# A mixture-of-experts loop with TensorE's order written out as a software pipeline

## The chip, the cores and the metric

One core of a Trainium2 chip runs a whole two-part transformer in float32. The metric is the device time of one execution in microseconds, from the core's first instruction to its last. The kernel before was run three times.

## The reference

The program is a first block (two layers with attention mixers and a dense feed-forward part) and a second block of two layers, each with a mixer and then sixteen experts. The change lies only in the experts of the second block. Sequence length there is L = 272 (256 tokens and 16 meta tokens), the width 1024, an expert's inner width 1408. Each expert takes the 34 tokens that score highest for it (expert choice), scaled by their score:

```
cap = EC_FACTOR * L // N_EXPERTS                 # 2 * 272 // 16 = 34
aff = jax.nn.softmax(jnp.einsum("bld,de->ble", u, router).astype(jnp.float32), axis=-1)
gates, idx = lax.top_k(jnp.swapaxes(aff, 1, 2), cap)
xs = jax.vmap(lambda ub, ib: ub[ib])(u, idx)
hid = jax.nn.silu(jnp.einsum("becd,edf->becf", xs, w1)) * jnp.einsum("becd,edf->becf", xs, w3)
ys = jnp.einsum("becf,efd->becd", hid, w2) * gates[..., None].astype(u.dtype)
return jax.vmap(lambda yb, ib: jnp.zeros((L, D), yb.dtype).at[ib].add(yb))(ys, idx)
```

The three weight matrices of an expert are read once from HBM; nothing is shared between experts.

## The kernel before

`second_block` keeps the residual x in SBUF, features on the partitions (8 chunks of 128 x 272). After each layer's mixer, `experts` (line 2185) computes the router, the 34 slots per expert as one-hot matrices `oh`, and the tokens with tokens on the partitions (`utok`, `utl`). Its loop (line 2364) then runs over the sixteen experts in four groups of four.

`gather` (line 2276) multiplies `utok` and `utl` with the one-hot matrices of a group and writes the group's tokens, scaled by the norm's gain, into one of two halves of `mixT` (`xs` in the code). It runs at once for a whole group before the group's first expert: 24 products in two rounds of two PSUM banks, each evicted by ScalarE or VectorE.

`one_expert` (line 2314) then does, in the order of the code:

- three parts j of the two up projections, 512, 512 and 384 columns wide. The gathered tokens (34 columns) are the stationary operand, the weight slabs the moving one; w1 goes to PSUM partitions 0 to 33, w3 to 64 to 97 of the same bank. ScalarE copies the one half to `hid` (line 2328), VectorE the other (line 2329);
- right behind each part, 3 or 4 transposes of `hid` on TensorE (`K.tr`, helper line 440), silu on ScalarE (2336) and the product on VectorE (2337) into `hT`;
- two small products that spread the slots and scores of the expert over the partitions (`sp`, `ap`), from which `pe`, the weighted one-hot matrix, is made (2343, 2345);
- the down projection: 11 row chunks, two products each, from three slabs (4, 4 and 3 chunks), evicted to `ys` (2354, 2355);
- the scatter: eight products of `ys` with `pe`, each added to a chunk of x by VectorE (2360). After the last expert each chunk of x is also squared on ScalarE (1208), and a product with ones adds the squares to `nst`, the sums that the next norm needs.

All products are issued through the helper at line 388, so the profile's lines are read by the names of their tiles: `bank<-w,mixT` is an up projection, `bank<-ca,hid` a transpose, `bank<-slT,ca` and `bank<-affT,ca` the two small products, `bank<-w,hT` the down projection, `bank<-pe,ys` the scatter, `bank<-oh,utok` and `bank<-oh,utl` the gather.

The weights come through `weights` (2303): every slab goes to the next slot of its size, seven slots of 2 MiB (`big`, lines 2390 to 2393, two of them in halves with a transfer each) and three of 1.5 MiB (`small`, line 2394). An expert uses six big and three small slabs. All are issued by SyncE from one queue (line 378), each waits until TensorE has read the slab that was in its slot, and none overtakes another. In layer 1's last expert the last slab comes in three pieces of 512 KB.

PSUM tiles come from one pool of eight banks. The order of each engine's instructions is set by the framework's scheduler; a `manual_schedule` around a piece of code keeps the named engines in the order of the code. In the mixers TensorE is held so; in the experts' loop nothing is (MS is 1, so the branch at the loop's head is not taken).

Of the kernel before, what the change touches and what calls it, by code (L numbers as in the profile page):

```python
# [2 lines left out]
L, S, D, KD = 272, 256, 1024, 8  # L3
# [24 lines left out]
# columns of the first mixer's input projection in units of 128, in the order of their use  # L28
# [3 lines left out]
# the second mixer's projections as w_in2 holds them  # L32
# [3 lines left out]
# mixer chunks in four passes of the output projection  # L36
# [104 lines left out]
def prep(I):  # L141
# [50 lines left out]
    for l in range(2):  # L192
        # two chunks of both halves to a slab
        for j in range(11):
            c = slice(256 * j, 256 * j + 256)
            fu.append(_slab(np.concatenate([up[l][:, :FF][:, c], up[l][:, FF:][:, c]], 1)).reshape(128, -1))
# [96 lines left out]
class Fill:  # L293
    """Work for the tensor engine that is handed out in small steps while another chain waits."""
# [26 lines left out]
    def piece(self):  # L321
        """one step; what it takes, or None when there is none to be had."""
# [18 lines left out]
class Kit:  # L341
# [15 lines left out]
    def widen(self, ctx, name, n, side="left", ring=None, size=4096, parts=1):  # L357
        """n more slots for the weight stream while ctx lasts, in one or more parts."""
# [23 lines left out]
    def load(self, src, n=4096):  # L382
        """a slab in the next slot."""
# [6 lines left out]
    def mm3(self, out, a, b, start=True, stop=True):  # L390
        """a^T b from exact two-part splits: high x high, high x low, low x high."""
# [4 lines left out]
    def split(self, src, a, into=None):  # L396
        """weights [128, a, b] as the exact sum of two parts of twelve significant bits."""
# [9 lines left out]
    def units(self, thunks, ahead=1):  # L407
        """split weights in turn, some units ahead of their use."""
# [7 lines left out]
    def cols(self, src, ms, nk=KD, width=512):  # L416
        """thunks for the 128-column chunks ms of a slab that is loaded at the first of them."""
# [9 lines left out]
    def rows(self, src):  # L427
        """thunks for pairs of the 128-row chunks of a slab of 512 columns."""
# [27 lines left out]
    def add_squares(self, st, k, sq):  # L456
        """adds the k-th of eight chunks of squares, over its features, to the token sums of column group k % 4."""
# [3 lines left out]
    def token_sums(self, st, tiles, g4):  # L461
        """the four groups' sums -> 32 x the sums with the tokens on the partitions, a column per tile."""
# [7 lines left out]
def first_block(K, tap):  # L470
# [5 lines left out]
    with ExitStack() as cx:  # L476
# [65 lines left out]
        def spread(r):  # L542
            """two columns of per-token values -> rows on all partitions, in PSUM [128, S]."""
# [8 lines left out]
        def pair_sums(st, p, src, dve=False):  # L552
            """adds the squares of the chunk pair p to the token sums."""
# [11 lines left out]
        def scale_of(st):  # L565
            """token sums -> 1 / rms on all partitions, in PSUM [128, S]."""
# [14 lines left out]
        def bank_out(st, z, p, bank, gp):  # L581
            """token sums of the squares of bank p, two 128-feature chunks, and the chunks times gp."""
# [6 lines left out]
        def post_norm(st, z, last=False):  # L589
            """x += z / rms(y), y of token sums st; the token sums of the new x."""  # L590
# [16 lines left out]
        def fm(us, hT, emit, n=4, nk=KD):  # L607
            """feature-major products for n units of 128 columns, two to a bank; emit(i, bank) per bank."""
# [21 lines left out]
        def tok_v(us, hT, dst):  # L630
            """token-major products [S, 512]: activations stationary, weights moving."""
# [25 lines left out]
        def scores_soft(sc_ps, G, n, biases, scale):  # L657
            """scores of G heads [128, G, n] in one PSUM bank -> normalised probabilities in SBUF."""
# [19 lines left out]
        def pv_heads(h, pr, v, heads, hh, o_ps):  # L678
            """o^T of heads 2 j + hh, j in heads (pairs of this bank), for query half h."""
# [15 lines left out]
        def o_out(oT, o_ps, m0, h):  # L695
            """the outputs of four head pairs for query half h, split."""
# [5 lines left out]
        def attend(score, bias, scale, v, base, oT, m0, waits):  # L702
            """softmax attention of four head pairs, the scores a step ahead of the rest."""
# [32 lines left out]
        def even_mixer(hT, oT, cy, bias):  # L736
# [42 lines left out]
        def odd_mixer(hT, oT, cy, c1v):  # L779
# [17 lines left out]
            def stick_a(zps, az):  # L797
                """scores and exp(-|scores|) of a step, a part per half of the heads."""
# [1631 lines left out]
```

## Time and profile before

| | us |
|---|---|
| median of 3 runs | 2753.06 |
| lowest, highest run | 2749.35, 2765.5 |
| profiled execution, span | 2750.4 |
| expert loop of layer 0, first product to last down product | 670.2 |
| expert loop of layer 1, likewise | 671.8 |
| TensorE busy, share of the span | 2482.9, 90% |
| VectorE busy, share of the span | 1084.4, 39% |
| ScalarE busy, share of the span | 755.7, 27% |

The profiled execution's own time is its span; it lies 2.7 us under the median. A busy matmul in the profile is not TensorE at its peak, since matmuls overlap and their ends are modelled; each float32 product appears as two records. PE is TensorE, PEld its weight load, DVE VectorE, ACT ScalarE, SP SyncE. "granted clock" or PEclk is the share of TensorE's full 2.4 GHz that it was given.

### The profile page before, as it was taken

To read this page: it belongs to the slowest core of one execution; us is meant where nothing else is said; L and a number is where in the kernel's file an instruction comes from. 1 tells how busy PE (TensorE), PEld (TensorE's weight loads), DVE (VectorE), ACT (ScalarE), POOL (GpSimd) and SP (SyncE) were. 2 spreads that over 40 slices of the span, in tenths; PEclk is the share of its full clock that TensorE was granted. 3 is DMA by queue.
4 is the path that set the end of the run, shared out by engine and by line. 5 is a ranking of instruction groups with operands and counts; after the bars stand their busy time and mean duration, and the time that the engine had idled before them with its cause. 6 is when DMAs were issued, how large, how long until landed. Compare 5 with 4: busy or idle time off the path is not lost. (4 is left out here: it accounts for less than half of the span.)

```text
span 2750.4 us, 43569 instructions
## 1 busy us (share of the span) xinstructions
PE 2482.9 (90%) x18599; PEld 1515.0 (55%) x18599; DVE 1084.4 (39%) x2308; ACT 755.7 (27%) x1471; POOL 206.9 (8%) x260
## 2 busy tenths in 40 slices
PE   6999998999989998898888988899988898888987
PEld 4779987689978784232232322588762232322322
DVE  3557766577675562111111111474641111111112
ACT  3445545355554341000010000342420000000001
POOL 0011011110032110000000000122100000000000
PEclk9999999999988999999999999898989999999998
DMA  9484443764132337999999998223169999999992
GB/s 360 161 370 179 171 160 118 314 268 154 45 94 63 117 135 301 425 425 380 422 381 426 414 392 353 86 69 117 71 241 397 424 388 425 386 389 423 388 425 100
DMA packets 78194, 753.43 MB, mean 274 GB/s; under 512 B 9600, under 2 KB 13584, under 8 KB 24624
## 3 DMA queue, kind: packets, MB, share of 16 engines
q1 hardware_dynamic: 75072, 748.38, 67.4%
q8 instruction: 146, 2.39, 0.3%
q10 hardware_dynamic: 2928, 2.26, 0.3%
q14 instruction: 48, 0.39, 0.0%
HBM read 749.54 MB, written 1.07 MB: 273 GB/s over the span
## 5 line engine op out<-in xcount | busy, mean ns | idle before, releaser
L388 PE MATMUL bank<-w,mixT 128*34 128x512 f32 (+1 forms) x3072 | 643.2, 573 | 0.0
L388 PEld LDWEIGHTS bank<-w,mixT 128*34 128x34 f32 x3072 | 176.7, 114 | 409.6 <-issue 393.9
L403 DVE TENSOR_TENSOR wlo<-w,whi 128x1024 fp32r<-128x1024 f32 (+1 forms) x242 | 298.9, 1237 | 168.6 <-ACT whi L401 167.3
L401 ACT ACTIVATE whi<-w 128x1024 fp32r<-128x1024 f32 x246 | 258.4, 1054 | 319.8 <-PE bank L388 125.5
L388 PE MATMUL bank<-w,hT 128*34 128x512 f32 x1408 | 330.8, 628 | 0.0
L2329 DVE COPY hid<-bank 34x512 f32<-34x512 f32 (+1 forms) x96 | 62.4, 650 | 627.7 <-ACT hid L2328 627.7
L388 PE MATMUL up<-hF,whi 128*128 128x256 f32 x1408 | 256.6, 285 | 5.2 <-ACT hF L573 5.2
L2328 ACT ACTIVATE hid<-bank 34x512 f32<-34x512 f32 (+1 forms) x96 | 53.2, 555 | 690.3 <-PE bank L388 690.3
L388 PEld LDWEIGHTS up<-hF,whi 128*128 128x128 f32 x1408 | 219.7, 192 | 6.8 <-ACT hF L573 5.9
L388 PEld LDWEIGHTS bank<-w,hT 128*34 128x34 f32 x1408 | 84.4, 117 | 229.9 <-issue 223.3
L388 PE MATMUL bank<-u,whi 128*128 128x272 f32 (+1 forms) x896 | 207.3, 324 | 2.5 <-ACT u L1293 2.3
L388 PE MATMUL up<-hF,wlo 128*128 128x256 f32 x704 | 199.4, 284 | 0.0
L440 PE MATMUL bank<-ca,hid 128*128 128x128 f32 x352 | 59.5, 288 | 131.2 <-DVE hid L2329 131.2
L388 PEld LDWEIGHTS bank<-u,whi 128*128 128x128 f32 (+1 forms) x896 | 148.1, 198 | 19.6 <-issue 6.9
L440 PEld LDWEIGHTS bank<-ca,hid 128*128 128x128 f32 x352 | 36.7, 140 | 211.3 <-DVE hid L2329 211.3
L2355 DVE COPY ys<-bank 34x512 f32<-34x512 f32 x32 | 22.2, 694 | 318.7 <-ACT ys L2354 318.7
L388 PE MATMUL bank<-u,wlo 128*128 128x272 f32 (+1 forms) x448 | 136.0, 304 | 5.5 <-DVE wlo L403 3.7
L388 PEld LDWEIGHTS up<-hF,wlo 128*128 128x128 f32 x704 | 134.4, 191 | 0.2
L388 PE MATMUL bank<-pe,ys 34*128 34x272 f32 x512 | 100.3, 433 | 22.3 <-ACT ys L2354 22.1
L452 POOL TENSOR_TENSOR rr<-rv,ca 128x3 f32<-128x3 f32 (+4 forms) x28 | 32.7, 1170 | 1027.9 <-DVE rv L450 1027.9
L2354 ACT ACTIVATE ys<-bank 34x512 f32<-34x512 f32 x32 | 18.9, 590 | 316.2 <-PE bank L388 316.2
L2360 DVE TENSOR_TENSOR x<-x,bank 128x272 f32<-128x272 f32 x256 | 95.4, 433 | 23.8 <-PE bank L388 21.0
(501 smaller groups left out, 3637.1 us busy)
## 6 DMA issues: line engine op xcount, KB each, us to landing
w<-in_ew SPq DMA_DIRECT2D x136, 2048.0 KB, 14.1
w<-in_ew SPq DMA_DIRECT2D x95, 1536.0 KB, 10.6
w<-in_ew SPq DMA_DIRECT2D x112, 1024.0 KB, 12.7
w<-in_ada SPq DMA_DIRECT2D x24, 2048.0 KB, 8.3
w<-in_ffn_up SPq DMA_DIRECT2D x22, 2048.0 KB, 8.4
w<-in_w_in SPq DMA_DIRECT2D x54, 512.0 KB, 3.6
w<-in_ffn_down SPq DMA_DIRECT2D x10, 2048.0 KB, 8.5
w<-in_ab_in SPq DMA_DIRECT2D x5, 2048.0 KB, 15.4
```

The costliest lines, as they stand in the source:

```text
L388: self.nc.tensor.matmul(out, lhsT, rhs, start=start, stop=stop, skip_group_check=True)
L401: self.nc.scalar.activation(v(hi[:, :n]), src, AF.Copy)
L403: (self.nc.gpsimd if self.splits in self.pool_share else self.nc.vector).tensor_tensor(v(lo[:, :n]), src, v(hi[:, :n].bitcast(F32)), op=OP ...
L440: self.nc.tensor.transpose(out, in_, self.ident[:k, :k] if n is None else n)
L452: nc.gpsimd.tensor_tensor(r[:, :n], v[:, :n], self.cst("half")[:, :n], op=OP.pow)
L2328: nc.scalar.activation(hb[0:CAP, :n], pu[0:CAP, :n], AF.Copy)
L2329: nc.vector.tensor_copy(hb[64:64 + CAP, :n], pu[64:64 + CAP, :n])
L2354: nc.scalar.activation(ys[0:CAP], py[0:CAP], AF.Copy)
L2355: nc.vector.tensor_copy(ys[64:64 + CAP], py[64:64 + CAP])
L2360: nc.vector.tensor_tensor(x[:, k], x[:, k], pc[:, :L], op=OP.add)
```

## The change

`one_expert` is cut into functions: `up` (one part of the up projections with its copies to `hid`), `turned` (the transposes of one part with silu and product), `places` (the two small products and `pe`), `down` (the products of one slab of w2) and `scatter`. The loop calls them in a new order and holds TensorE to it with `manual_schedule`; the other engines are still ordered by the scheduler. The transposes of part 0 come behind part 1, those of part 1 behind part 2, those of part 2 behind the first slab of the down projection. The scatter of an expert comes behind part 0 of the next. `gather` does half of its work per call; both halves for group 0 stand ahead of the loop, those for a later group inside experts 1 and 2 of the group before. `nst` takes its bank after the loop instead of before it.

```diff
-            def gather(g):
+            def gather(g, k0):
                 hot = [oh[:, t, 4 * g:4 * g + 4].rearrange("p e c -> p (e c)") for t in range(3)]
-                for k0 in (0, 2):
-                    pg = [K.bank() for _ in range(2)]
+                pg = [K.bank() for _ in range(2)]
...
-            nst = K.bank("nst")
-
-            def one_expert(e):
...
+            def up(ex, e, j, n, off):
+
+                ws = [weights(A[m][l, e, :, off:off + 8 * n], 8, n) for m in ("ew1", "ew3")]
+                pu = K.bank()
...
+                nc.scalar.activation(hb[0:CAP, :n], pu[0:CAP, :n], AF.Copy)
+                nc.vector.tensor_copy(hb[64:64 + CAP, :n], pu[64:64 + CAP, :n])
+                ex["hid", j] = hb
+
+            def turned(ex, j, n):
+
+                pt, nf, hb = K.bank(), n // 128, ex.pop(("hid", j))
+                for f in range(nf):
+                    K.tr(pt[:, 128 * f:128 * f + 128], hb[:, 128 * f:128 * f + 128])
...
+            def scatter(ex, nst=None):
+
                 for n, k in enumerate((0, 4, 1, 5, 2, 6, 3, 7)):
                     r = slice(64 * (k // 4), 64 * (k // 4) + CAP)
                     pc = K.bank()
-                    K.mm(pc[:, :L], ys[r, 128 * (k % 4):128 * (k % 4) + 128], pe[r])
+                    K.mm(pc[:, :L], ex["ys"][r, 128 * (k % 4):128 * (k % 4) + 128], ex["pe"][r])
                     nc.vector.tensor_tensor(x[:, k], x[:, k], pc[:, :L], op=OP.add)
-                    if e == NE - 1:
+                    if nst is not None:
                         square_sums(K, Y.tile([128, L], F32, name="nsq"), nst, n, k)
 
-            for e in range(NE):
-                if e % 4 == 0:
-                    gather(e // 4)
-                with ExitStack() as co:
-                    if MS > 1 and e == 0:
-                        co.enter_context(tc.manual_schedule(engines={mybir.EngineType.SP}))
-                    one_expert(e)
+            offs = [8 * sum(widths[:j]) for j in range(3)]
+            prev = None
+            with tc.manual_schedule(engines={mybir.EngineType.PE}):
+                for k0 in (0, 2):
+                    gather(0, k0)
+                for e in range(NE):
+
+                    ex = {"hT": Y.tile([128, 11, CAP], F32, name="hT")}
+                    up(ex, e, 0, widths[0], offs[0])
+                    if prev is not None:
+                        scatter(prev)
+                    up(ex, e, 1, widths[1], offs[1])
+                    turned(ex, 0, widths[0])
+                    places(ex, e)
+                    up(ex, e, 2, widths[2], offs[2])
+                    turned(ex, 1, widths[1])
+                    if e % 4 in (1, 2) and e < NE - 4:
+                        gather(e // 4 + 1, 2 * (e % 4 - 1))
+                    down(ex, e, 0, 4)
+                    turned(ex, 2, widths[2])
+                    down(ex, e, 4, 4)
+                    for f0, n in ((8, 3),) if e < NE - 1 or l == 0 else ((8, 1), (9, 1), (10, 1)):
+                        down(ex, e, f0, n)
+                    prev = ex
+                nst = K.bank("nst")
+                scatter(prev, nst)
             return nst
```

On TensorE, in the kernel before, from the down projection of expert 2 of layer 0 through expert 3 to the gather of the second group, the instructions stand so:

```order
L388 MATMUL bank<-w,hT 34x512 x22
L388 MATMUL bank<-pe,ys 128x272 x8
L388 MATMUL bank<-w,mixT 34x512 x16
L440 MATMUL bank<-ca,hid_11698 128x128 x4
L388 MATMUL bank<-w,mixT 34x512 x16
L440 MATMUL bank<-ca,hid_11699 128x128 x4
L388 MATMUL bank<-w,mixT 34x384 x16
L440 MATMUL bank<-ca,hid_11700 128x128 x3
L388 MATMUL bank<-slT,ca 128x272
L388 MATMUL bank<-affT,ca 128x272
```

Then follow the 22 products of the down projection, the 8 of the scatter and the gather's 8, 4, 8 and 4. Each group of transposes reads the `hid` that the products right ahead of it have just filled.

On TensorE, in the changed kernel, expert 1 of layer 0 from the scatter of expert 0 on (its own part 0 stands right ahead):

```order
L388 MATMUL bank<-pe,ys 128x272 x8
L388 MATMUL bank<-w,mixT 34x512 x16
L440 MATMUL bank<-ca,hid_11698 128x128 x4
L388 MATMUL bank<-slT,ca 128x272
L388 MATMUL bank<-affT,ca 128x272
L388 MATMUL bank<-w,mixT 34x384 x16
L440 MATMUL bank<-ca,hid_11699 128x128 x4
L388 MATMUL bank<-oh,utok 128x136 x8
L388 MATMUL bank<-oh,utl 128x136 x4
L388 MATMUL bank<-w,hT 34x512 x8
L440 MATMUL bank<-ca,hid_11700 128x128 x3
L388 MATMUL bank<-w,hT 34x512 x14
```

Every group of transposes now has a part or a slab's products between itself and the products that filled its `hid`, and half of the next group's gather stands in the middle of the expert.

At the end of layer 0, TensorE's scatter of the last expert with the sums of squares (`nst`), in the kernel before:

```order
L388 MATMUL bank<-pe,ys 128x272
L388 MATMUL nst<-nsq,ca 32x272
L388 MATMUL bank<-pe,ys 128x272 x4
L388 MATMUL nst<-nsq,ca 32x272
L388 MATMUL bank<-pe,ys 128x272
L388 MATMUL nst<-nsq,ca 32x272
L388 MATMUL bank<-pe,ys 128x272 x2
L388 MATMUL nst<-nsq,ca 32x272 x5
```

Four of the scatter's products go ahead together in one place, and the last five sums stand at the end.

The same place in the changed kernel, with the numbers of the buffers:

```order
L388 MATMUL bank_14519<-pe_14446,ys_14515 128x272
L388 MATMUL nst_14518<-nsq_14522,ca_65 32x272
L388 MATMUL bank_14525<-pe_14446,ys_14515 128x272
L388 MATMUL nst_14518<-nsq_14528,ca_65 32x272
L388 MATMUL bank_14531<-pe_14446,ys_14515 128x272
L388 MATMUL nst_14518<-nsq_14534,ca_65 32x272
```

Five more such pairs follow: product and sum now take strict turns, eight times. SyncE issues the experts' transfers in the same order as before.

## Rows read from the trace of the kernel before

**Rows 1.** The page's rate of the transfers, in 40 equal slices of the span.

```profile
GB/s 360 161 370 179 171 160 118 314 268 154 45 94 63 117 135 301 425 425 380 422 381 426 414 392 353 86 69 117 71 241 397 424 388 425 386 389 423 388 425 100
```

**Rows 2.** Windows (stretch, length; PE, PEld, DVE, ACT, POOL busy; PEclk; DMA share; GB/s).

```profile
1065.40:1735.60 670.20, 594.16 (x2868) 203.78 (x2864) 112.34 (x262) 60.73 (x142) 1.49 (x8) 0.96 0.93 387
2053.40:2725.20 671.80, 595.72 (x2866) 204.76 (x2864) 112.13 (x261) 60.74 (x142) 0.00 (x0) 0.96 0.92 384
1100.00:1220.00 120.00, 105.63 (x509) 34.56 (x507) 20.89 (x48) 10.42 (x24) 0.00 (x0) 0.97 1.01 425
```

**Rows 3.** DMA issues of the experts' weights: times, KB each, us to landing.

```profile
w<-in_ew SPq DMA_DIRECT2D x136, 2048.0 KB, 14.1
w<-in_ew SPq DMA_DIRECT2D x95, 1536.0 KB, 10.6
w<-in_ew SPq DMA_DIRECT2D x112, 1024.0 KB, 12.7
...
w<-in_ew SPq DMA_DIRECT2D x3, 512.0 KB, 4.7
```

**Rows 4.** Timeline of TensorE, expert 0 of layer 0 (start, length, what).

```profile
1065.45 7.06 PE L388 MATMUL bank<-w,mixT 128*34 128x512 f32 x32
...
1074.02 0.66 PE L440 MATMUL bank<-ca,hid 128*128 128x128 f32 x4 [1.51 <-DVE hid L2329]
...
1083.70 5.36 PE L388 MATMUL bank<-w,mixT 128*34 128x384 f32 x32
1090.32 0.55 PE L440 MATMUL bank<-ca,hid 128*128 128x128 f32 x3 [1.27 <-DVE hid L2329]
...
1091.90 9.64 PE L388 MATMUL bank<-w,hT 128*34 128x512 f32 x44
1102.23 2.83 PE L388 MATMUL bank<-pe,ys 34*128 34x272 f32 x16 [0.69 <-ACT ys L2354]
1104.99 1.48 PE L388 MATMUL bank<-w,mixT 128*34 128x512 f32 x6
```

**Rows 5.** SyncE's waits from 1065 to 1740 us: total, times, longest.

```profile
SPq L378 <- PE bank L388: 581.5, 88, 24.5
```

**Rows 6.** TensorE's waits from 1065.4 to 1735.6 us: total, times, longest.

```profile
PE bank L440 <- DVE hid L2329: 65.6, 48, 1.5
PE bank L388 <- ACT ys L2354: 10.4, 15, 0.7
```

**Rows 7.** Windows at a loop's start, after a gather, and at its end.

```profile
1060.00:1080.00 20.00, 18.49 (x102) 8.46 (x102) 2.25 (x6) 3.43 (x7) 0.00 (x0) 0.93 0.70 270
1080.00:1100.00 20.00, 17.29 (x89) 5.71 (x87) 2.32 (x5) 2.01 (x5) 0.00 (x0) 1.00 0.87 343
...
1240.00:1260.00 20.00, 15.90 (x85) 5.41 (x81) 2.81 (x6) 2.48 (x6) 0.00 (x0) 1.00 0.86 342
...
1700.00:1720.00 20.00, 17.13 (x84) 5.10 (x82) 1.98 (x4) 1.75 (x4) 0.86 (x7) 0.97 0.43 167
```

**Rows 8.** Timeline of TensorE, second half of the second group's gather.

```profile
1230.94 2.12 PE L388 MATMUL bank<-oh,utok 128*128 128x136 f32 x16
1232.99 0.73 PE L388 MATMUL bank<-oh,utl 32*128 32x136 f32 x8
1233.65 0.63 PE L388 MATMUL bank<-w,mixT 128*34 128x512 f32 x2
```

**Rows 9.** Timeline of TensorE at the end of the layers.

```profile
1725.99 9.64 PE L388 MATMUL bank<-w,hT 128*34 128x512 f32 x44
...
2725.86 0.72 PE L388 MATMUL bank<-pe,ys 34*128 34x272 f32 x2 [0.69 <-ACT ys L2354]
...
2731.20 1.27 PE L388 MATMUL bank<-pe,ys 34*128 34x272 f32 x2
...
2733.44 1.27 PE L388 MATMUL bank<-pe,ys 34*128 34x272 f32 x2
...
2738.52 1.44 PE L388 MATMUL nst<-nsq,ca 128*32 128x272 f32 x4 [0.51 <-ACT nsq L1208]
```

More of the change, by code (lines that the diff above doesn't have):

```diff
@@ new lines, in gather @@
+                pg = [K.bank() for _ in range(2)]
+                for i in range(2):
+                    for q in range(2):
+                        k = k0 + i + 4 * q
+                        for t in range(2):
+                            K.mm(pg[i][:, 136 * q:136 * q + 136], utok[:, t, 128 * k:128 * k + 128], hot[t],
+                                 start=t == q == 0, stop=False)
+                for q in range(2):
+                    for i in range(2):
+                        j = 32 * (k0 + i)
+                        K.mm(pg[i][:, 136 * q:136 * q + 136], utl[j:j + 32, 128 * q:128 * q + 128], hot[2][j:j + 32],
+                             start=False)
@@ L2300, in experts @@
+                for q in range(2):
+                    for i in range(2):
+                        k = k0 + i + 4 * q
+                        o, ps = xs[:, g % 2, k], pg[i][:, 136 * q:136 * q + 136]
+                        if i == 0:
+                            nc.scalar.activation(o, ps, AF.Copy, scale=n2[:, k:k + 1])
+                        else:
+                            nc.vector.tensor_scalar(o, ps, n2[:, k:k + 1], None, op0=OP.mult)
             turn = [0]
@@ new lines, in up @@
+            def up(ex, e, j, n, off):
+                ws = [weights(A[m][l, e, :, off:off + 8 * n], 8, n) for m in ("ew1", "ew3")]
+                pu = K.bank()
+                r = slice(CAP * (e % 4), CAP * (e % 4) + CAP)
+                for k in range(KD):
+                    for i, w in enumerate(ws):
+                        K.mm(pu[64 * i:64 * i + CAP, :n], xs[:, e // 4 % 2, k, r], w(k), start=k == 0, stop=k == KD - 1)
+                hb = hid[turn[0] % HID]
+                turn[0] += 1
+                nc.scalar.activation(hb[0:CAP, :n], pu[0:CAP, :n], AF.Copy)
+                nc.vector.tensor_copy(hb[64:64 + CAP, :n], pu[64:64 + CAP, :n])
+                ex["hid", j] = hb
@@ new lines, in turned @@
+            def turned(ex, j, n):
+                pt, nf, hb = K.bank(), n // 128, ex.pop(("hid", j))
+                for f in range(nf):
+                    K.tr(pt[:, 128 * f:128 * f + 128], hb[:, 128 * f:128 * f + 128])
+                pv = pt[:, :n].rearrange("p (f c) -> p f c", f=nf)
+                sl = Y.tile([128, 4, CAP], F32, name="sl")
+                nc.scalar.activation(sl[:, :nf], pv[:, :, 0:CAP], AF.Silu)
+                nc.vector.tensor_tensor(ex["hT"][:, 4 * j:4 * j + nf], sl[:, :nf], pv[:, :, 64:64 + CAP], op=OP.mult)
@@ L2338, in one_expert, with places @@
+            def places(ex, e):
                 sp = K.bank()
@@ L2343, in one_expert, with down @@
                 nc.scalar.activation(ab, ap[:, :L], AF.Copy)
-                pe = Y.tile([128, L], F32, name="pe")
-                nc.vector.scalar_tensor_tensor(pe, sp[:, :L], K.cst("iotap"), ab, op0=OP.is_equal, op1=OP.mult)
-                py = K.bank()
-                for f0, n in ((0, 4), (4, 4), (8, 3)) if e < NE - 1 or l == 0 else ((0, 4), (4, 4), (8, 1), (9, 1), (10, 1)):
-                    w = weights(A["ew2"][l, e, :, f0:f0 + n].rearrange("p f n -> p (f n)"), n, 1024)
-                    for f in range(n):
-                        for i in range(2):
-                            K.mm(py[64 * i:64 * i + CAP, :], hT[:, f0 + f], w(f)[:, 512 * i:512 * i + 512],
-                                 start=f0 + f == 0, stop=f0 + f == 10)
-                ys = Y.tile([128, 512], F32, name="ys")
-                nc.scalar.activation(ys[0:CAP], py[0:CAP], AF.Copy)
-                nc.vector.tensor_copy(ys[64:64 + CAP], py[64:64 + CAP])
+                ex["pe"] = Y.tile([128, L], F32, name="pe")
+                nc.vector.scalar_tensor_tensor(ex["pe"], sp[:, :L], K.cst("iotap"), ab, op0=OP.is_equal, op1=OP.mult)
+            def down(ex, e, f0, n):
+                if f0 == 0:
+                    ex["py"] = K.bank()
+                py = ex["py"]
+                w = weights(A["ew2"][l, e, :, f0:f0 + n].rearrange("p f n -> p (f n)"), n, 1024)
+                for f in range(n):
+                    for i in range(2):
+                        K.mm(py[64 * i:64 * i + CAP, :], ex["hT"][:, f0 + f], w(f)[:, 512 * i:512 * i + 512],
+                             start=f0 + f == 0, stop=f0 + f == 10)
+                if f0 + n == 11:
+                    ys = ex["ys"] = Y.tile([128, 512], F32, name="ys")
+                    nc.scalar.activation(ys[0:CAP], py[0:CAP], AF.Copy)
+                    nc.vector.tensor_copy(ys[64:64 + CAP], py[64:64 + CAP])
+            def scatter(ex, nst=None):
                 for n, k in enumerate((0, 4, 1, 5, 2, 6, 3, 7)):
```

41 lines of the change are left out of this document (removed).

## The prediction

> **What bounds the kernel now.** I read the page's slices first: the rate of the transfers stands near 400 to 426 GB/s in two long stretches of the span and far below that elsewhere [rows 1]. Those stretches are the expert loops of the two layers of the second block, the only part that the change touches. The table of windows then gives each loop as one row: from the first product of expert 0 to the end of expert 15's last product it is 670.2 us in layer 0 and 671.8 us in layer 1, with TensorE at a granted clock of 0.96 and a mean of 387 and 384 GB/s [rows 2]. In a stretch without a gather the rate is 425 GB/s with the DMA engines busy all the time (share 1.01) [rows 2]. So two resources are nearly level here and the question is which one ends an expert.
>
> Work it out for both. The DMA issues for `in_ew` are 136 of 2048 KB, 95 of 1536, 112 of 1024 and 3 of 512 [rows 3]: 540,672 KB, or 276.8 MB per layer and 17.3 MB per expert. At 425 GB/s an expert takes 40.7 us. The timeline of TensorE in expert 0, at full clock, shows 39.5 us from its first product to the first product of expert 1 [rows 4]. The gathers of the three later groups and the half-clock stretches come on top: 670/16 is 41.9 us per expert. So TensorE's own chain is what ends an expert, by about one microsecond over the transfers. That agrees with the wait tables: SyncE waited 581.5 us for TensorE to release a weight buffer [rows 5], while TensorE's own list of waits is led by 65.6 us in 48 waits for `hid`, 1.37 us each and three per expert, and 10.4 us in 15 waits for `ys` [rows 6]: TensorE stands still while ScalarE and VectorE copy what it is about to transpose or scatter.
>
> A second cost is less visible. The buffers hold seven slabs of 2 MiB and three of 1.5 MiB, 19.4 MB, a little more than one expert. They are full when expert 0 begins. As TensorE is the slower one, they stay as full as the releases allow, and at the end of the layer the transfers stop early: from 1700 to 1720 us the rate is already 167 GB/s while products run until 1735.6 [rows 2, 7]. That drain is time in which the layer's scarcest resource does nothing.
>
> **The change, part by part.** *The waits.* Transposes stand one part later and the scatter stands behind the next expert's first part. What is between is a part of 5.4 to 7.1 us [rows 4], against copies that TensorE awaited for 1.3 to 1.5 us, or 0.7 us for `ys` [rows 4, 6]. The cover is several times the wait, so I count all three waits and the `ys` wait as gone: 3 x 1.4 + 0.7 = 4.9 us per expert, leaving 39.5 - 4.9 = 34.6 us. If a copy were late after all, what stands behind it on TensorE is one whole part. The third transpose has the thinnest cover: it stands behind the first eight products of the down projection, 8/22 of 9.64 = 3.5 us, against 1.3 [rows 4].
>
> *The gather.* The same 24 products per group now come as two halves of 12, inside experts 1 and 2 of the group before. A half took 2.7 us at full clock (1230.94 to 1233.65) [rows 8]. TensorE's work does not shrink, but the ScalarE and VectorE evictions behind it lie beside products, and TensorE no longer arrives at a new group with all releases late: after the gather at 1227 the rate fell to 342 GB/s for 20 us [rows 7]. Three gathers of 5.4 us are 16 us per layer.
>
> *TensorE's new sum* is 16 x 34.6 + 16 = 570 us per layer at full clock, against about 606 us that the transfers need (next). The order of the two is reversed: what is late next is the weight transfer, and TensorE waits for slabs.
>
> *The transfers' sum.* 276.8 - 19.4 = 257.4 MB remain at the first product, at 425 GB/s 605.7 us. They cannot begin before a buffer is released: half a slab halfway through the first part, 1065.4 + 3.5 = 1069 us. Until the pipeline of releases is full there are gaps; in the kernel before, the windows from 1060 to 1100 us run at 270 and 343 GB/s [rows 7]. With the releases of parts 1 and 2 now about 2 us earlier I put the gaps at 5 us (bounds: 0, and 11 us, the whole shortfall of these two windows against 425: 3.1 + 1.6 MB). That gives the last byte at 1069 + 605.7 + 5 = 1680 us. Behind it come the landing and the products that still stand: the last slab has 3 of 11 row chunks, 2.6 us of 9.64, and about 3 us for landing and for what TensorE has left of the slabs before (bounds 2 and 8). So the last product of layer 0 ends near 1686 instead of 1735.6: **50 us less**. The same length of 620.6 us from 2053.4 in layer 1 ends at 2674 instead of 2725.2: **51 us less** [rows 9]. The three small last slabs of layer 1 wait for part 2 of the last expert as they did; eleven microseconds of products lie over their transfer, 0.5 MB each.
>
> *The tail.* After the last expert, the scatter and the sums of squares are now in strict turn: one scatter product, then the sum that needs VectorE's add and ScalarE's square of it, then the next. Before, four scatter products went ahead in one place and two in another. A single turn took 2.24 us (2731.20 to 2733.44) [rows 9]; eight turns are 18 us, where the whole took 14.1 us (2725.86 to 2739.96) [rows 9]. This wait is added; behind it on TensorE stand all later scatter products, and the next layer or the output waits for the last. I take +4 us per layer (bounds 0, and +10 if in layer 0 VectorE's weight splitting falls between the adds).
>
> *Costs put at nothing.* The transfers are issued in the same order, so the buffers' turns do not change; the first mixer's weights of layer 1 still wait for TensorE's releases. One more PSUM bank is free during the loop, since the sums' bank is taken only at its end. ScalarE and VectorE have 61 and 112 us of work in 670 [rows 2], so their new order has slack.
>
> *Sum.* 50 + 51 - 2 x 4 = 93 us. The profiled span of 2750.4 becomes 2657. The median of the runs lies 2.7 us above that span, so I predict **2660 us**.
>
> **Two rules of the Trainium skill weighed.** The rate that carries the sum is 425 GB/s over 120 us with one core at work [rows 2]. The Trainium skill's page DMA: Bandwidth & Descriptors (section Where 436 GB/s comes from) says that loads from HBM are bound near 358 GB/s per core, and sets 435 as the fabric's ceiling. By 358 the 257.4 MB would take 719 us, more than the loop takes now, and the change could win nothing; by 435 they take 592 us and each layer ends 14 us earlier than I say. The trace disagrees with the lower figure and lies just under the upper one, so the measurement decides.
>
> The granted clock was 0.96 over the loops, so of 670 us about 54 were at half clock [rows 2], and this with TensorE never short of weights. The Trainium skill's page TensorE: Matmul & The Clock Gate (section Loop structure matters more than you think) speaks against this change: a loop that waits for a transfer before its products lets the engine fall to the lower clock. That is rival B, whose price follows from rows.
>
> **Rivals.** *A, the forecast:* the transfers end the layer. Its own range comes from 420 to 430 GB/s (about 7 us per layer either way), the gaps and the tail: 2644 to 2682.
>
> *B: the clock.* Waiting for slabs, TensorE runs at 1.2 GHz more often. At half clock, work takes twice as long; TensorE's 570 us may lose 50 us per layer before it is later than the transfers, which is 100 us at half clock, twice today's 54. Today's idle time, 670 - 594 = 76 us, made those 54 us [rows 2], and the new idle time is smaller (620 - 570 = 50 us, some 3 us per expert, spread over nine slabs); when the clock falls, the waits vanish and with them the cause. If it lost 75 us instead, the layers would end 25 us later each: 2710.
>
> *C: the queue runs dry.* SyncE issues in one order, and the loads of part 2 wait for part 2 of the expert before, with others behind them. If this left gaps so that the mean was 405 GB/s, the transfers would take 30 us more per layer: 2720. Against it: 425 was held for 120 us at a time with the same order and later releases.
>
> *D, slower:* once TensorE is starved, each slab's landing and its products follow one another instead of overlapping, because the hand-made order lets nothing pass the waiting product. An expert then costs 40.7 us plus what is uncovered. It decides from 1.2 us per expert (41.9 now); three uncovered waits of 1.5 us would be 45.2 us and 53 us per layer more: about 2870. Against it: ten slots ahead keep the queue filled when TensorE is the one that waits.
>
> **How the numbers follow.** A 0.79, B 0.09, C 0.07, D 0.03, and 0.02 that the transfers were the limit already and nothing changes. What can be told from no change here is about 1%, 27 us. A and most of B and C are faster by more: 0.93 faster, 0.04 the same, 0.03 slower. The range holds A and a good part of B and C: 2643 to 2705.
>
> **What would show it.** In the profile after: waits for `hid` and `ys` nearly gone from TensorE's list and waits for `in_ew` in their place, some 40 us or more per layer; the rate at 425 GB/s without the dips after gathers and until about 6 us before the last product; loops of about 620 us; the last scatter with its sums about 18 us. I am wrong if the clock in the loops falls below 0.9, if the rate stays under 410 with SyncE waiting for releases throughout, or if `hid` still leads the waits.

## The result and the profile after

| | before | after |
|---|---|---|
| median of 4 runs, us | 2751.2 | 2675.68 |
| lowest, highest run, us | 2748.42, 2765.5 | 2670.22, 2680.31 |
| profiled execution, span, us | 2750.4 | 2668.5 |
| mean granted clock of the span | 0.942 | 0.948 |

The ratio is 0.9709, with a 95% interval of 0.9675 to 0.9743: faster by 2.9%. The forecast was 2660 us in a range of 2643 to 2705; the median lies in it, 16 us above the forecast. The rate of the transfers, in the page's 40 slices, is the first thing to look at:

```profile
GB/s 366 145 366 221 174 167 127 267 301 190 20 106 73 114 81 229 389 426 424 426 426 424 425 425 425 157 81 55 92 233 372 425 425 424 426 425 425 426 424 166
```

In [rows 1] the two loops show 380, 381, 392, 388, 386, 389 between slices of 425. Now every slice that lies wholly in a loop, behind its first, stands at 424 to 426, and the rate falls away at once behind it. The windows after give the two loops, two stretches inside the first, the tails behind the loops, the end of the second loop's transfers, and the mixer between the loops (columns as in [rows 2]):

```profile
1065.40:1686.60 621.20, 582.27 (x2868) 197.59 (x2864) 112.33 (x262) 60.26 (x142) 1.55 (x8) 0.98 1.00 418
2011.10:2632.50 621.40, 582.19 (x2867) 199.30 (x2864) 112.04 (x261) 60.25 (x142) 0.00 (x0) 0.97 0.99 415
1100.00:1220.00 120.00, 120.00 (x635) 43.60 (x632) 26.10 (x62) 13.00 (x31) 0.00 (x0) 1.00 1.01 425
1240.00:1260.00 20.00, 17.14 (x74) 5.26 (x76) 3.66 (x9) 0.59 (x1) 0.00 (x0) 0.83 1.01 427
1686.60:1712.30 25.70, 17.03 (x32) 4.99 (x32) 6.49 (x11) 5.95 (x12) 0.18 (x1) 0.58 0.29 97
2626.00:2628.00 2.00, 2.00 (x12) 0.59 (x12) 0.26 (x1) 0.26 (x1) 0.00 (x0) 1.00 0.35 143
2628.00:2630.00 2.00, 2.00 (x12) 0.59 (x10) 0.00 (x0) 0.00 (x0) 0.00 (x0) 1.00 0.00 0
2632.50:2658.20 25.70, 17.03 (x32) 4.99 (x32) 4.19 (x9) 4.09 (x10) 0.00 (x0) 0.58 0.00 0
1712.30:2011.10 298.80, 276.68 (x3634) 234.15 (x3634) 187.00 (x446) 124.51 (x283) 59.68 (x74) 0.90 0.33 120
```

The loops went from 670.2 and 671.8 us to 621.2 and 621.4. From 1100 to 1220 us TensorE did 635 records' work where it did 509 [rows 2], without an idle moment in the profile, while the transfers ran at the same 425 GB/s. Then the transfers took over: from 1240 to 1260 us, behind the first gather's old place, the rate holds 427 where it was 342 [rows 7], and TensorE is the one with gaps. At the end of layer 1, where no later layer's weights are in the queue, the transfers last into the window from 2626 to 2628 us, 5 to 6 us ahead of the end of the last product at 2632.5. Before, the rate was down to 167 GB/s from 1700 to 1720 us, with 16 us of the loop still to come [rows 7].

The waits of TensorE after, from 1065 to 1690 us (total, times, longest):

```profile
PE bank L388 <- DMA w<-in_ew: 38.9, 19, 4.6
PE nst L388 <- ACT nsq L1208: 1.0, 1, 1.0
PE bank L388 <- ACT ys L2359: 0.7, 1, 0.7
```

The 48 waits for `hid` are gone, and so are the `ys` waits of the loop; the one left belongs to the tail [rows 6]. TensorE now waits for weights instead: 582.3 us busy and 38.9 us waiting are the loop's 621.2. SyncE's waits in the same stretch:

```profile
SPq L378 <- DMA w<-in_ew: 406.0, 123, 5.0
SPq L378 <- PE bank L388: 140.7, 38, 24.5
```

SyncE waited 581.5 us for TensorE's releases [rows 5]; now it is 140.7, and it waits 406.0 us for earlier transfers: buffers come free faster than the transfers can use them. Accordingly each transfer spends longer in the queue (KB each, us from issue to landing):

```profile
w<-in_ew SPq DMA_DIRECT2D x136, 2048.0 KB, 28.3
w<-in_ew SPq DMA_DIRECT2D x95, 1536.0 KB, 27.1
w<-in_ew SPq DMA_DIRECT2D x112, 1024.0 KB, 28.5
```

Against 14.1, 10.6 and 12.7 us [rows 3] the landings take twice as long or more, at a rate that is no lower.

Inside an expert the timeline of TensorE (1447 to 1473 us: end of part 0, scatter of the expert before, part 1, transposes of part 0, part 2, transposes of part 1, start of a gather) reads:

```profile
1447.28 7.05 PE L388 MATMUL bank<-w,mixT 128*34 128x512 f32 x30 [1.75 <-DMA w<-in_ew]
1454.27 2.10 PE L388 MATMUL bank<-pe,ys 34*128 34x272 f32 x16
1456.30 7.06 PE L388 MATMUL bank<-w,mixT 128*34 128x512 f32 x32
1463.30 0.65 PE L440 MATMUL bank<-ca,hid 128*128 128x128 f32 x4
1464.99 5.36 PE L388 MATMUL bank<-w,mixT 128*34 128x384 f32 x32
1470.28 0.65 PE L440 MATMUL bank<-ca,hid 128*128 128x128 f32 x4
1470.77 2.02 PE L388 MATMUL bank<-oh,utok 128*128 128x136 f32 x16
```

Neither the scatter nor the transposes carry a wait any more; in [rows 4] the transposes waited 1.51 and 1.27 us and the scatter 0.69. The one bracket left names a slab.

Where did the 81.9 us of the span come from? The loops gave 49.1 and 50.5. The tails, from the last down product to the last sum, took 25.65 us each instead of 14.1 and 14.8: 11.5 and 10.9 us given back. The mixer of layer 1 between the loops took 298.8 instead of 303.6 us, though nothing in it was changed. 49.1 + 50.5 - 11.5 - 10.9 + 4.8 is 82.0.

What was open then: whether the transfers are what ends the loop now; which of the three moves the loop's gain needs; and why the tail cost three times the forecast.

### The profile page after: what moved, and what is told of

Read it like the earlier page. It is cut to its first block, busy times and chain, and to the rows that moved or that the text cites. A ratio compares the mean times of both kernels' runs of the same rounds, so it can differ in the third digit from the quotient of the medians.

```text
span 2668.5 us, 43625 instructions
## 1 busy us (share of the span) xinstructions
PE 2462.9 (92%) x18599; PEld 1502.2 (56%) x18599; DVE 1084.4 (41%) x2308; ACT 755.4 (28%) x1471; POOL 207.2 (8%) x260
## 5 line engine op out<-in xcount | busy, mean ns | idle before, releaser
L388 PE MATMUL bank<-w,mixT 128*34 128x512 f32 (+1 forms) x3072 | 683.2, 578 | 78.1 <-DMA w<-in_ew 78.1
L388 PEld LDWEIGHTS bank<-w,mixT 128*34 128x34 f32 x3072 | 188.3, 115 | 540.0 <-issue 402.9
L388 PE MATMUL bank<-w,hT 128*34 128x512 f32 x1408 | 314.6, 595 | 0.0
L388 PEld LDWEIGHTS bank<-w,hT 128*34 128x34 f32 x1408 | 77.8, 112 | 189.2 <-issue 187.3
L388 PE MATMUL acc<-gh,wlo 128*128 128x256 f32 x352 | 99.1, 282 | 0.0
L388 PE MATMUL acc<-gh,whi 128*128 128x256 f32 x352 | 99.0, 281 | 0.0
L388 PE MATMUL acc<-gl,whi 128*128 128x256 f32 x352 | 99.0, 281 | 0.0
L388 PE MATMUL bank<-hT,whi 128*128 128x256 f32 (+1 forms) x464 | 88.9, 294 | 7.7 <-ACT hT L573 3.1
```

The source lines that it names most:

```text
L388: self.nc.tensor.matmul(out, lhsT, rhs, start=start, stop=stop, skip_group_check=True)
```

## The experiments

Each takes the changed kernel and edits one thing. Where single executions are compared, the loops are compared and not the totals, since the changed kernel's own runs differ by 10 us. "Loop" is the stretch from the first up product to the last down product.

**no_scatter.** If TensorE no longer ends an expert, work taken from it must gain nothing.

```diff
                     up(ex, e, 0, widths[0], offs[0])
-                    if prev is not None:
-                        scatter(prev)
                     up(ex, e, 1, widths[1], offs[1])
```

> Leaves out the scatter of experts 0 to 14 with its adds to x; only expert 15 is scattered. TensorE has 15 x 2.8 = 41 us less to do per layer. Theory (the transfers end the loop): the loops stay at 621 us within 3, the waits for weights grow by about 40 us per layer. Rival (TensorE's work still ends the loop): the loops fall to 580 to 590 us, the span by 60 to 80.

Measured: 2673.17 us, loops of 623.3 and 623.7. Window and wait of layer 0's loop:

```profile
1064.60:1687.90 623.30, 560.59 (x2626) 176.96 (x2624) 67.99 (x142) 60.56 (x142) 1.55 (x8) 0.95 0.99 416
```

```profile
PE bank L388 <- DMA w<-in_ew: 62.0, 28, 5.3
```

240 records of TensorE's work are gone and the loop is no shorter. TensorE's busy time fell by 21.7 us, and its waits for weights rose by 23.1 us, from 38.9 to 62.0. That is little more than half of the 40 us expected: a scatter in the changed kernel's loop is 2.10 us long (1454.27 above) and not the 2.8 of the kernel before, 15 of them 31.5 us, and the granted clock fell too, 0.98 to 0.95, so that the work left took longer. The loop is not TensorE's to shorten.

**fewer_bytes.** The other side of the same question: take bytes from the transfers and leave TensorE all its products.

```diff
-                w = weights(A["ew2"][l, e, :, f0:f0 + n].rearrange("p f n -> p (f n)"), n, 1024)
+                if f0 < 8:
+                    w = ex["w2"] = weights(A["ew2"][l, e, :, f0:f0 + n].rearrange("p f n -> p (f n)"), n, 1024)
+                else:
+                    w = lambda f, b=f0 - 8: ex["w2"](b + f)
```

> Leaves out the transfer of the third slab of w2 of every expert (its products read the second slab again): 25.2 MB or 59 us of transfers less per layer, TensorE's work unchanged. Theory (transfers end the loop of the changed kernel, TensorE's sum is about 570 us): loops fall until TensorE ends them, to 572 to 595 us, and the waits for weights nearly vanish. Rival (something else than the bytes sets 621 us): loops above 610.

Measured: 2588.91 us, loops of 569.2 and 569.1.

```profile
1070.10:1639.30 569.20, 562.51 (x2866) 199.22 (x2864) 112.34 (x262) 60.22 (x142) 1.55 (x8) 1.00 0.99 414
```

```profile
PE bank L388 <- DMA w<-in_ew: 6.7, 4, 2.2
```

With 16 x 1.573 = 25.2 MB fewer per layer, 59 us at 425 GB/s, the loop is 52 us shorter, a little below the 572 to 595 expected. It stops there because TensorE is busy for 562.5 us of 569.2, at full clock. So TensorE's own sum for a layer, which the forecast put at 570 us, is 562.5 us, or 569 with the waits that are left, and the transfers of the changed kernel stand some 52 us above it. Together with no_scatter this shows that the transfers end the loop now.

**turn_at_once.** One of the moves undone: each part's transposes stand right behind it again, and the two small products behind the third.

```diff
                     up(ex, e, 0, widths[0], offs[0])
+                    turned(ex, 0, widths[0])
...
                     up(ex, e, 1, widths[1], offs[1])
-                    turned(ex, 0, widths[0])
-                    places(ex, e)
-                    up(ex, e, 2, widths[2], offs[2])
                     turned(ex, 1, widths[1])
+                    up(ex, e, 2, widths[2], offs[2])
+                    turned(ex, 2, widths[2])
+                    places(ex, e)
...
                     down(ex, e, 0, 4)
-                    turned(ex, 2, widths[2])
```

> Only the move of the transposes is undone: each part's transposes stand right behind it, the two small products behind the third; the scatter still stands in the next expert and the gather is still in halves. Theory (the waits for hid carried the gain): 48 waits of 1.4 us come back, 66 us per layer, TensorE's sum is again about 640 us at full clock, the loops are 645 to 662 us and the span 2720 to 2750. Rival (the scatter's and the gather's moves or the order as such carried it): loops within 10 us of 621, span below 2690.

Measured: 2732.02 us, loops of 646.0 and 642.9.

```profile
1065.90:1711.90 646.00, 580.36 (x2866) 201.89 (x2864) 111.72 (x262) 60.86 (x142) 1.49 (x8) 0.96 0.96 402
```

```profile
PE bank L440 <- DVE hid L2323: 65.6, 48, 1.5
```

The wait for `hid` is back to the tenth of a microsecond and as often as in [rows 6], and 580.4 + 65.6 is the whole loop: TensorE ends it again, and no wait for weights is left. Undoing this move costs 22 to 25 us per layer, of the 65.6 us that it removed. In place of the rest the changed kernel waits for slabs, 38.9 us.

**scatter_at_once** and **gather_whole.** The other two moves undone, one at a time: the scatter right behind its own expert (but for the last, which stays where it is), and the whole gather ahead of each group.

```diff
-                    if prev is not None:
-                        scatter(prev)
...
                     prev = ex
+                    if e < NE - 1:
+                        scatter(ex)
```

> Only the scatter's move is undone: it stands right behind its expert's down projection. 15 waits of 0.7 us for ys come back, 10 us of TensorE's time per layer, which the waits for weights have room for. Theory (the transfers end the loop): loops 621 to 627 us, waits for weights smaller by about 10 us, span within 10 of the changed kernel's 2668.5 after the mixers' differences. Rival (each move counts on its own): loops 10 us longer, 631 to 635.

```diff
-                for k0 in (0, 2):
-                    gather(0, k0)
                 for e in range(NE):
+                    if e % 4 == 0:
+                        for k0 in (0, 2):
+                            gather(e // 4, k0)
...
-                    if e % 4 in (1, 2) and e < NE - 4:
-                        gather(e // 4 + 1, 2 * (e % 4 - 1))
```

> Only the gather's halving is undone: a group's whole gather stands ahead of its first expert, still in the hand-made order, and the scatter of the expert before comes behind the first part. Theory (the transfers end the loop): loops 621 to 627 us. Rival (the dips of the transfers after a gather in the kernel before were the gather's own): the rate falls below 400 in the windows after each gather and the loops are 635 or more.

Measured: 2681.0 us with loops of 623.1 and 623.2, and 2676.88 us with loops of 622.9 and 623.3. TensorE's waits with the scatter undone:

```profile
PE bank L388 <- DMA w<-in_ew: 27.1, 14, 4.5
PE bank L388 <- ACT ys L2359: 10.4, 15, 0.7
```

And with the gather undone:

```profile
PE bank L388 <- DMA w<-in_ew: 36.8, 16, 6.2
```

Neither shows a cost: the loops are at most 2 us longer than in the changed kernel's profile, and the same loop, unedited, took 622.9 to 623.5 us in the profiles of the two runs on the tail below. Nor does the gather's rival hold: in the 20 us behind each of the three later gathers the transfers run at 420, 428 and 425 GB/s, so the dips of the kernel before were not the gather's own. With the scatter undone the 10.4 us of `ys` waits return as they were [rows 6], and the waits for weights shrink by 11.8 us from 38.9: TensorE loses the time at one place and no longer loses it at another. The two moves were not undone together. The total of 2681.0 us is not a cost of the edit in the loop: this execution's loop 0 began at 1073 us instead of 1065, behind stages that it shares with the changed kernel.

**all_at_once.** All three moves undone, but TensorE's order still held by hand. Is it the holding that gains, or does it cost?

```diff
-                for k0 in (0, 2):
-                    gather(0, k0)
                 for e in range(NE):
+                    if e % 4 == 0:
+                        for k0 in (0, 2):
+                            gather(e // 4, k0)
...
                     up(ex, e, 0, widths[0], offs[0])
-                    if prev is not None:
-                        scatter(prev)
-                    up(ex, e, 1, widths[1], offs[1])
                     turned(ex, 0, widths[0])
-                    places(ex, e)
-                    up(ex, e, 2, widths[2], offs[2])
+                    up(ex, e, 1, widths[1], offs[1])
                     turned(ex, 1, widths[1])
-                    if e % 4 in (1, 2) and e < NE - 4:
-                        gather(e // 4 + 1, 2 * (e % 4 - 1))
-                    down(ex, e, 0, 4)
+                    up(ex, e, 2, widths[2], offs[2])
                     turned(ex, 2, widths[2])
+                    places(ex, e)
+                    down(ex, e, 0, 4)
...
                     prev = ex
+                    if e < NE - 1:
+                        scatter(ex)
```

> All three moves are undone while TensorE is still held to the order of the code, so the loop stands as in the kernel before. Theory (the moves, not the holding, made the gain): loops 666 to 675 us as before, the strict tail of 25.7 us stays, span 2755 to 2780. Rival (the scheduler's order was the trouble): loops below 650.

Measured: 2787.19 us, loops of 673.7 and 671.8, tails of 26.4 and 26.0. The span of 2785.5 us lies beyond the 2780 expected, with layer 1's mixer at 311.8 us instead of 298.8.

```profile
1065.40:1739.10 673.70, 597.56 (x2866) 204.74 (x2864) 112.29 (x262) 60.72 (x142) 1.49 (x8) 0.95 0.93 385
```

The loops are those of the kernel before, 670.2 and 671.8. Holding the order gains nothing by itself; the moves do. Whether they need the holding was not tried. And the tail of 26 us came with the holding alone. The parts don't add: undone alone they leave the first loop 25, 2 and 2 us longer, undone together 52. As long as the transposes stand late, the transfers end the loop and hide what either of the other two would cost. With the transposes at once TensorE ends it, and undoing the other two as well costs 28 us more (646.0 to 673.7).

**tail_free.** Now the tail. The last scatter and its sums are taken out of the region in which TensorE's order is held, and nothing else.

```diff
                     prev = ex
-                nst = K.bank("nst")
-                scatter(prev, nst)
+            nst = K.bank("nst")
+            scatter(prev, nst)
```

> The last expert's scatter and its sums are left to the scheduler again, as in the kernel before; the loop stays in the hand-made order. Theory (the strict turns of product, add, square and sum cost the tail): the stretch from the last down product to the last sum falls from 25.7 us to the 14 to 15 us of the kernel before in both layers, and the span from 2668.5 to about 2646. Rival (the tail is long because TensorE is at half clock after a loop that waited for transfers, whatever the order): the stretch stays above 20 us and the span above 2658.

Measured: median 2662.33 us (2660.91 to 2667.12, 4 runs), ratio to before 0.9661, 0.9605 to 0.9716. The tails took 13.6 and 10.5 us instead of 25.65 twice: 27 us of tails gone, as the loops stood at 622.9 and 623.5. In the profiled execution (span 2660.2) only 8 us of it arrive: the loops took 4 us more together, the first began 3 us later, and layer 1's mixer took 12 more. So the span misses the 2646 expected and lies above the 2658 named for the rival. The stretches, which are the edit's own, speak against the rival: they lie far under its 20 us. The two tails and that mixer as windows:

```profile
1691.80:1705.40 13.60, 10.68 (x34) 3.22 (x32) 6.11 (x11) 5.73 (x11) 0.18 (x1) 0.66 0.55 180
2639.90:2650.40 10.50, 7.79 (x32) 2.83 (x32) 3.93 (x9) 3.84 (x9) 0.00 (x0) 1.00 0.00 0
1705.40:2016.30 310.90, 287.80 (x3634) 243.40 (x3634) 186.61 (x446) 125.13 (x283) 59.54 (x74) 0.86 0.32 116
```

The tails are 3 us apart, one at a granted clock of 0.66, the other at 1.00. In the mixer the same 3634 records as after took 310.9 us at 0.86, against 298.8 at 0.90. What lowered the clock there was not tried.

**tail_ahead.** The tail still held by hand, but with the scatter's products three ahead of the sums, so that the add and the square of one chunk lie beside the products of the next. The squares take turns under two names of buffers, since up to four of them are alive at a time.

```diff
-                scatter(prev, nst)
+                late = deque()
+                for n, k in enumerate((0, 4, 1, 5, 2, 6, 3, 7)):
+                    r = slice(64 * (k // 4), 64 * (k // 4) + CAP)
+                    pc = K.bank()
+                    K.mm(pc[:, :L], prev["ys"][r, 128 * (k % 4):128 * (k % 4) + 128], prev["pe"][r])
+                    nc.vector.tensor_tensor(x[:, k], x[:, k], pc[:, :L], op=OP.add)
+                    sq = Y.tile([128, L], F32, name=("nsq", "ab")[n % 2])
+                    nc.scalar.activation(sq, x[:, k], AF.Square)
+                    late.append((n, sq))
+                    if len(late) > 3:
+                        K.add_squares(nst, *late.popleft())
+                while late:
+                    K.add_squares(nst, *late.popleft())
```

> The last scatter is held in a hand-made order in which its products run three ahead of the sums. Theory of the strict turns: product, add and square of different chunks overlap, so the stretch falls below that of the kernel before, to 11 to 13 us per layer, and the span to about 2642. Rival (half clock): above 20 us per layer and a span above 2658.

Measured: median 2641.16 us (2637.48 to 2642.65, 4 runs), ratio to before 0.9577, 0.9531 to 0.9623, an interval wholly below that of the change as it stands. The tails took 9.2 us each. Layer 0's tail as a window, and the start and end of layer 1's on TensorE's timeline:

```profile
1690.40:1699.60 9.20, 8.05 (x32) 2.98 (x32) 6.29 (x11) 5.64 (x12) 0.18 (x1) 1.00 0.58 199
```

```profile
2622.63 1.91 PE L388 MATMUL bank<-pe,ys 34*128 34x272 f32 x8 [0.69 <-ACT ys L2359]
2624.47 0.65 PE L388 MATMUL nst<-nsq,ca 128*32 128x272 f32 x2
2625.04 0.72 PE L388 MATMUL bank<-pe,ys 34*128 34x272 f32 x2
...
2630.44 0.65 PE L388 MATMUL nst<-ab,ca 128*32 128x272 f32 x2 [0.40 <-ACT ab L2404]
```

Four products go ahead; from then on product and sum follow each other without a wait, 1.2 us a pair, and only the last sum waits 0.40 us. It is the fastest of all versions: the span of 2640.9 lies 27.6 us under that of the change, and the two tails are 33 us of it, of which the loops (623.2 and 622.9) and a later start of the first loop take back some 5.

## Why the prediction was right, and where it was off

**The bound.** The forecast said that TensorE's chain ended an expert by a microsecond over the transfers, and that the transfers would end it once the waits were gone. Shown: without the moves 597.6 us of work and 76 of waits are TensorE's whole loop (all_at_once); with them, removing TensorE's work changes nothing and removing bytes does.

**The waits.** The 4.9 us per expert of `hid` and `ys` waits went as said; none is left in the loop. The third transposes with the thinnest cover don't wait either. One gain was not counted: behind the next expert's first part the scatter itself takes 2.10 us (1454.27 above) instead of 2.83 [rows 4]. What was late next was the slabs, with 38.9 us of waits against the "some 40 us or more" named beforehand.

**The transfers' sum.** 605.7 us of transfers, 3.5 of start, 5 of gaps and 6 of landing and last products gave 620.6 us; the loops took 621.2 and 621.4, and layer 0's last product ended at 1686.6 where 1686 was forecast. Its smaller terms hold too. The transfers of layer 1 ended 5 to 6 us ahead of the last product, against about 6. The loop's start shows in finer windows:

```profile
1065.40:1068.90 3.50, 3.50 (x20) 0.99 (x18) 0.62 (x2) 0.64 (x2) 0.00 (x0) 1.00 0.01 5
1068.90:1075.00 6.10, 6.10 (x32) 1.72 (x30) 0.69 (x1) 0.59 (x1) 0.00 (x0) 1.00 0.72 235
...
1080.00:1090.00 10.00, 10.00 (x57) 3.68 (x56) 2.35 (x5) 2.70 (x6) 0.00 (x0) 1.00 0.94 364
```

Next to nothing moves (5 GB/s) for the 3.5 us until half of the first part is done. Then 235 GB/s for 6.1 us and 364 for 10 us are 2.7 and 1.4 us short of 425: 4.1 us of gaps, against 5.

**TensorE's sum** of 570 us was 562.5 of work in a loop of 569.2 (fewer_bytes). That it comes so near is in part luck: the 0.7 us per expert by which the scatter became shorter is missing from the forecast, and 6.7 us of the 569.2 are waits for weights.

**The rivals in the loop.** B, the clock: it rose from 0.96 to 0.98 and 0.97. TensorE's waits in the loop, 19 in 621 us and 4.6 us at most, did not hold it down, though single stretches did fall (0.83 from 1240 to 1260 us), and with still more waiting it fell further (0.95 in no_scatter). The Trainium skill's page TensorE: Matmul & The Clock Gate (section Loop structure matters more than you think) warns of long waits for transfers between products; the loops here don't bear it out at a size that costs anything, while the tail, below, shows a fall of that kind beside another sort of wait. C, a dry queue: 424 to 426 GB/s in every whole slice of the loops behind the first. D, uncovered landings: landings of 28 us stood wholly under other transfers.

**The term that was off: the tail.** The step reads: "A single turn took 2.24 us (2731.20 to 2733.44) [rows 9]; eight turns are 18 us", so +4 us per layer. It was +11.5 and +10.9, a little past its bound of +10. The profiled span of 2668.5 is 11.5 us over the 2657 of the sum: 14.4 from the tails and 1.4 from the loops, less the mixer's 4.8, with half a microsecond not assigned. The other 4 us of the miss are that this execution was the fastest of four: the median lies 7.2 us above its span, where I took 2.7. The timeline of layer 1's tail after shows what a turn is:

```profile
2633.15 0.72 PE L388 MATMUL bank<-pe,ys 34*128 34x272 f32 x2 [0.69 <-ACT ys L2359]
2634.86 0.65 PE L388 MATMUL nst<-nsq,ca 128*32 128x272 f32 x2 [0.99 <-ACT nsq L1208]
2635.44 0.72 PE L388 MATMUL bank<-pe,ys 34*128 34x272 f32 x2
...
2638.19 1.27 PE L388 MATMUL bank<-pe,ys 34*128 34x272 f32 x2
2639.50 0.44 DVE L2368 TENSOR_TENSOR x<-x,bank 128x272 f32<-128x272 f32 x1 [2.87 <-PE bank L388]
2639.97 0.43 ACT L1208 ACTIVATE nsq<-x 128x272 f32<-128x272 f32 x1 [2.88 <-DVE x L2368]
2640.46 1.11 PE L388 MATMUL nst<-nsq,ca 128*32 128x272 f32 x2 [0.99 <-ACT nsq L1208]
2641.50 1.27 PE L388 MATMUL bank<-pe,ys 34*128 34x272 f32 x2
```

The first turn takes 2.29 us (2633.15 to 2635.44): product, add, square, sum, each waiting for the one before. Then the granted clock falls, the product lasts 1.27 instead of 0.72 us, and a turn takes 3.31 (2638.19 to 2641.50); the tail's windows show 0.58. The 2.24 us of [rows 9] had no such wait in it. There TensorE was at half clock already (the product took 1.27 us) and did a product and the sum of an earlier chunk back to back: two products' worth of time, and no chain. I read the period of a pipelined stretch as the latency of a chain that was not in the trace of before. That eight turns of 2.24 nearly give the length which the tail would have at full clock, 0.7 + 8 x 2.29 = 19 us (an estimate from the first turn), is luck. The other 6.7 of the 25.65 us are the turns at half clock, about 1 us longer each, and rival B had priced the clock for the loops alone. That the strict turns are the cause is shown from two sides: without the holding the tail is 13.6 and 10.5 us, and held by hand with the products ahead it is 9.2, at a clock of 1.00. A loop that waited for transfers is not the cause: in fewer_bytes the loop ran at 1.00 with 6.7 us of such waits, and its tails, in strict turns, still took 26.3 and 25.7 us at 0.57.

**Costs put at nothing.** Transfer order, the freed PSUM bank and the slack of ScalarE and VectorE: no run shows a cost in any of them, and no wait of TensorE in the loop but that for slabs is left.

## What to carry to other kernels

When two resources are nearly level, removing one's waits pays only down to the other's sum, so work out both: here TensorE's own loop fell by 101 us (670.2 to 569.2 in fewer_bytes) and 49 arrived. Where another resource ends the loop, undoing one move at a time understates what the moves gain together.

A region whose order is held by hand should not take in a reduction at its end in which each step needs three engines in turn; let the products run a few steps ahead of the sums. And the period of a row that repeats is a chain's latency only if the instruction waits for its own predecessor: look for the wait in brackets before multiplying by it.

## What was not expected of the hardware

The granted clock was 1.00 shortly before the tail (2628 to 2630 us) and 0.58 over it, where TensorE waited 0.99 us in each turn: the first product ran at full clock and from the second sum on everything ran at 1.2 GHz. With the same products and sums issued three ahead it stayed at 1.00. Where the framework's scheduler set the order, with two to four waits for a square in a tail, it was 0.66 and 1.00 in the two tails of tail_free, and 0.61 in both of the kernel before:

```profile
1735.60:1749.80 14.20, 11.68 (x34) 3.71 (x32) 6.11 (x11) 5.74 (x12) 0.18 (x1) 0.61 0.52 173
```

So the fall at the tail was there before the change, where the forecast's rows already stood at half clock; what decides it in the scheduler's order stays open.

Layer 1's mixer, the same in all versions, took 298.8 us at a granted clock of 0.90, 303.6 at 0.88 and 310.9 at 0.86:

```profile
1749.80:2053.40 303.60, 280.66 (x3635) 237.21 (x3635) 187.19 (x446) 124.41 (x283) 59.54 (x74) 0.88 0.33 118
```

That row is of the kernel before; those of the others stand above. Twelve microseconds between versions can thus lie in a stage that none of them touched, more than some of the effects looked for here, so stages were compared and not totals. What sets the clock in that stage stays open.

Twice the time from issue to landing, 28 against 14 us, came with an undiminished 425 GB/s. Landing time alone would have looked like slower transfers; the rate shows that they were not.
